# Sums over partitions as four 32-column matmuls, attention spread over all eight convolutions, y's parts made inside the last one

## The chip, the cores and the metric

The kernel runs on one core of a Trainium2 chip. The metric is the device time of one execution in microseconds (us), and lower is better. Where this text speaks of engines, PE is the matrix engine (TensorE), PEld its weight loads, DVE the vector engine, ACT the scalar engine, POOL the GpSimd engine and SP the engine that issues most DMAs. A time that differs by less than 0.2% (4.4 us) cannot be told from no change by this measurement.

## The reference

One transformer block for 512 tokens of width 2048 in float32: a normalised and modulated input goes through one wide projection. A third of the projection's columns feed a gated short convolution, the rest a sparse attention. Both outputs are normalised in groups of 128 channels, concatenated, multiplied by `w_out`, gated by `g_a` and added to `x`; a gated feed-forward network (FFN) follows.

```python
sh_a, sc_a, g_a, sh_f, sc_f, g_f = split(silu(c) @ ada_w + ada_b, 6)      # 6 x 2048 columns
h = rms_norm(x, norm_mix) * (1 + sc_a) + sh_a
proj = h @ w_in                                # 512 x 5656
cb, cc, ch, q, kc, vc, ... = split(proj)       # cb, cc, ch: 1024 columns each
u = cc * ch
y_conv = cb * (causal convolution over 3 tokens of u with conv_w)
y_conv = rms_norm(y_conv in 8 groups of 128 channels) * out_norm_conv
y_attn = nsa_mixer(...)                        # 8 heads of 128
y_attn = rms_norm(y_attn per head) * out_norm_attn
x = x + g_a * (concat(y_conv, y_attn) @ w_out)            # w_out 2048 x 2048
h = rms_norm(x, norm_ffn) * (1 + sc_f) + sh_f
x = x + g_f * ((silu(h @ ffn_w1) * (h @ ffn_w3)) @ ffn_w2)
```

## The kernel before

Every float32 product of the projection, of `w_out` and of the FFN is made of three faster matmuls: an operand is split into a high part (`hi`, rounded on ACT) and a low part (`lo`, the rest, subtracted on DVE), and hi·lo, lo·hi and hi·hi are summed in PSUM (`mm3`, L98 to L100). Small products (attention's scores, values and transposes, sums over partitions) are plain float32 matmuls, which the trace shows as two records each.

The stage that the change touches runs from the eight convolutions to the end of `w_out`.

- `conv(c)`, for c from 0 to 7, computes 128 channels of the three gates for all tokens. Its loop goes over 16 chunks of `w_in` in 8 steps of two: SP loads the raw chunk, ACT rounds it (L814), DVE makes its low part (L815, a ring of 3 buffers), and PE does 18 matmuls into three `main` banks. Behind the loop stand the convolution itself on DVE (L826 to L831, L831 being the last reader of the third bank), a square on ACT (L834), the sum of the squares over the 128 partitions by a matmul with a matrix of ones (L836, 512 columns, the sum in all 128 rows), a square root on ACT and a reciprocal on DVE over 128x512 (L123, L124), and the scaling of y (L840).
- `attention_steps()` is a list of 40 steps, of which 37 hold work: scores, softmax, transposes (L769), values (L778), the norm of a head and its turn into `oT` (L798). `weave(..., 0.68)` gives 0.68 of such a step to each of the 64 convolution steps. At that rate the 37 steps are used up in the seventh convolution, and the eighth has none beside it.
- `gates_beside()` multiplies columns of `ada_w` by the conditioning vector on DVE (L190, 128x512 each, from a ring of two buffers `araw` that SP fills) in 152 steps, 2.4 of them beside each convolution step. Where a part of the gate is wanted as a row or in all partitions, its accumulator is summed over partitions by a matmul with ones: L413 (one output row, for the FFN's gate `gfd`, four times, three of them in this stage and one in the fourth `w_out` block) and L211 (`ada_bcast`, all 128 rows, for each of the four `w_out` blocks).
- Then y, in 16 chunks of 128 channels (0 to 7 from the convolutions in `yc`, 8 to 15 from attention in `oT`), is split into its parts, 32 ACT casts (L864) and 32 DVE subtractions (L866) of 128x256. Those of chunks 0 to 6 are tied behind the last convolution's end by `issue_after`.
- `w_out` runs in four blocks of 512 output columns, each over 8 pairs of chunks (24 matmuls a pair), in the order 8 to 15, 0 to 7, with four `main` banks. `beside_block` accumulates the next block's gate beside it and calls `ada_bcast` for its own, and `residual` uses that at the block's end.

There are four `main` and four `aux` PSUM banks. The instructions are recorded in the order of the code and then moved by a scheduler inside the framework, engine by engine; so the order on an engine is not the order of the code. The FFN behind `w_out` takes the rest of the time and is not touched.

Of the kernel before, what the change touches and what calls it, by code (L numbers as in the profile page):

```python
# [9 lines left out]
F32 = mybir.dt.float32  # L10
# [3 lines left out]
ALU = mybir.AluOpType  # L14
# [55 lines left out]
def block_kernel(ctx: ExitStack, tc: tile.TileContext, a: dict, out: bass.AP):  # L70
# [134 lines left out]
            g0 = at[("norm_mix", "norm_ffn")[which]] + k0  # L205
            nc.vector.scalar_tensor_tensor(d, d, 1.0, cols[:, g0:g0 + n], op0=ALU.add, op1=ALU.mult)

    def ada_bcast(psum_tile, dst, acc):

        ps = psum_tile()  # L210
        nc.tensor.matmul(ps, ones, acc, start=True, stop=True)  # L211
        nc.scalar.copy(dst, ps)

    pp = pool("ps", 4, space=PSUM)
    main = lambda: pp.tile([P, S], F32, tag="main", name="main")
# [180 lines left out]

    dram = ctx.enter_context(tc.tile_pool(name="spill", bufs=1, space=bass.MemoryType.DRAM))
    gfd = dram.tile([1, D], F32, name="gfd")
    wst = ExitStack()
    wring = pool("aring", 2, stack=wst)  # L400

    def ffn_part(ring_, width, j):

        got = []
        if j < 8:
            m, j = 1 - j % 2, j // 2
            yield from ada(ring_, width, (3 + m) * D + j * 512, 512, got)
            ada_cols(aux, got[0], 1, m, 4 * j, 4)
        else:
            cs = slice((j - 8) * 512, (j - 7) * 512)  # L410
            yield from ada(ring_, width, 5 * D + cs.start, 512, got, bias=True)
            ps = aux()
            nc.tensor.matmul(ps[0:1, :], ones[:, 0:1], got[0], start=True, stop=True)  # L413
            nc.scalar.copy(got[0][0:1, :], ps[0:1, :])
            nc.gpsimd.dma_start(gfd[:, cs], got[0][0:1, :])
        yield

    def ffn_parts(ring_, width, js):
# [120 lines left out]
    def h_tok(k, i):  # L539
        return [h[:, i * P:(i + 1) * P] for h in hT[k]]  # L540

    every = list(range(KC))


    cst = ExitStack()
# [252 lines left out]
        nc.vector.tensor_mul(oT[:, g * R:(g + 1) * R, i * P:(i + 1) * P], pt.rearrange("p (h t) -> p h t", h=R), gain)  # L798


    conv_ins = [None]

    def conv(c):
        pst = {b: main() for b in (1, 2, 0)}
        for k in range(0, KC, 2):
            raw = ring[0].tile([P, 1024], F32, tag="raw", name="raw")
            hi = ring[1].tile([P, 1024], F32R, tag="hi", name="whi")
            lo = ring[2].tile([P, 1024], F32R, tag="lo", name="wlo")
            m = 2 * 3 * P
            src = w_in[k * P:(k + 2) * P, 0:3 * 1024].rearrange("(k p) (b n) -> p k b n", p=P, b=3)  # L810
            rv = raw[:, :m].rearrange("p (k b n) -> p k b n", k=2, b=3)
            for kk in range(2):
                nc.sync.dma_start(rv[:, kk], src[:, kk, :, c * P:(c + 1) * P])
            nc.scalar.copy(hi[:, :m], raw[:, :m])  # L814
            nc.vector.tensor_sub(lo[:, :m], raw[:, :m], hi[:, :m].bitcast(F32))  # L815
            for b in (1, 2, 0):
                for kk in range(2):
                    s = slice((kk * 3 + b) * P, (kk * 3 + b + 1) * P)
                    mm3(pst[b], [hi[:, s], lo[:, s]], hT[k + kk], k + kk == 0, k + kk == KC - 1)
            yield  # L820
# [10 lines left out]
        conv_ins[-1] = nc.vector.tensor_mul(y, y, pst[0]).ins  # L831

        sq = ap_.tile([P, S], F32, tag="cc", name="cc", bufs=1)
        nc.scalar.activation(sq, y, AF.Square)  # L834
        ps = aux()
        nc.tensor.matmul(ps, ones, sq, start=True, stop=True)  # L836
        rs = ap_.tile([P, S + 2], F32, tag="u", name="u", bufs=1)[:, :S]
        rsqrt(rs, ps, P)
        gain = cols[:, at["out_norm_conv"] + c:at["out_norm_conv"] + c + 1]
        nc.vector.scalar_tensor_tensor(y, y, gain, rs, op0=ALU.mult, op1=ALU.mult)  # L840

    def convs():
        for c in range(8):
# [6 lines left out]
        yield from ada(wring, 512, 2 * D, 512, acc_g, bias=True)  # L850

    later = gates_beside()
    weave(beside(convs(), later, 2.4), attention_steps(), 0.68)
    for _ in later:
        pass

    HS, HK = S // 2, KC // 2
    yT = [None] * KC
    for k in list(range(8, KC)) + list(range(8)):
        src = oT[:, k - 8, :] if k >= 8 else yc[:, k, :]  # L860
        yT[k] = parts()
        for h, t in enumerate(yT[k]):
            part = src[:, h * HS:(h + 1) * HS]
            nc.scalar.copy(t[:, 0:HS], part)  # L864
            with tc.issue_after(conv_ins[-1]) if k < 7 else ExitStack():
                nc.vector.tensor_sub(t[:, HS:S], part, t[:, 0:HS].bitcast(F32))  # L866
    at_.close()
    qk.close()
    wst.close()
# [58 lines left out]
    def beside_block(n, ga):  # L928

        own = acc_g[-1]  # L930
        side = ffn_part(aring, 1024, 11)
        if n < 3:
            side = ada(aring, 1024, 2 * D + (n + 1) * 512, 512, acc_g, bias=True)
        for t, _ in enumerate(after_taken(side)):
            if t == 0:
                if n:
                    x2_turned(n - 1)
                ada_bcast(aux, ga, own)
                if 0 < n < 3:
                    x_load(n + 1)  # L940
            yield
# [90 lines left out]
    for n in range(4):  # L1032
        ga = tp.tile([P, 512], F32, tag="ga", name="ga")
        pst = [main() for _ in range(NT)]
        if n < 3:
            weave(token_block(w_out, n * 512, y_tok, every[8:] + every[:8], pst), beside_block(n, ga), 1)
            residual(n, ga, pst, range(NT))

    def first_half():
# [5 lines left out]

    rbs = dp.tile([P, S], F32, tag="d1", name="rbs")

    weave(last_block_steps(every[8:] + every[:8], pst, first_half), beside_block(3, ga), 2)
    residual(3, ga, pst, range(2, NT))

    def second_half():
# [555 lines left out]
```

## Time and profile before

| what | value |
|---|---|
| median of three runs | 2211.52 us (2209.48 to 2212.58) |
| the profiled execution: its own time | 2209.06 us |
| its span, first to last instruction | 2207.3 us |
| mean granted PE clock | 0.997 of full speed |
| PE, DVE, ACT, POOL busy, share of the span | 98%, 78%, 45%, 10% |
| convolutions and attention, from the first whole step to the first `w_out` matmul | 312 to 721.4 us of the span |
| four `w_out` blocks | 721.4 to about 925 us |

The trace is one execution. Its busy times are those of the records; a PE record's end is modelled, so starts of neighbouring matmuls, not lengths, tell what a matmul costs. An engine works through its instructions in order: whatever stands behind a waiting instruction waits too.

### The profile page before, as it was taken

Reading aid. Unit: us, or ns where it says so; the run is one execution under the profiler, and the core shown is the slowest. Engines: PE = TensorE matmul, PEld = TensorE weight load, DVE = VectorE, ACT = ScalarE, POOL = GpSimd, SP = SyncE. Lnnn points to the kernel's source line nnn. Section 1 sums busy time; section 2 is a strip of 40 time slices with the busy share of each in tenths; the row PEclk is TensorE's granted clock in tenths of the full one; section 3 lists DMA queues with packets and bytes.
Section 4 is the critical chain, followed back from the end, with each engine's and each line's share of the span. In section 5 each row is a group of like instructions: output and inputs, shape, how many; then the busy total and the mean of one; then the engine's idle time right before and its main releaser. Section 6 shows DMA issues by size and latency. Waiting matters only on the chain.

```text
span 2207.3 us, 30666 instructions
## 1 busy us (share of the span) xinstructions
PE 2162.6 (98%) x11393; PEld 1807.2 (82%) x11393; DVE 1731.6 (78%) x2561; ACT 1002.4 (45%) x1594; POOL 225.9 (10%) x273
## 2 busy tenths in 40 slices
PE   6999999999999999999999999999999999999999
PEld 5778777778777788888888888888888887888887
DVE  6777868887877656698778888788788887878788
ACT  5335234555444333654444444444444455454543
POOL 5310000000000000000000000000000112121110
PEclk9999999999999999999999999999999999999999
DMA  9965775645547766269777677777677499797975
GB/s 319 363 232 160 244 234 172 179 147 169 159 142 244 207 244 223 86 160 222 174 185 177 175 170 170 177 186 174 173 167 175 97 314 275 161 292 145 290 161 143
DMA packets 437722, 435.21 MB, mean 197 GB/s; under 512 B 18084, under 2 KB 344588, under 8 KB 436932
## 3 DMA queue, kind: packets, MB, share of 16 engines
q1 hardware_dynamic: 368196, 318.47, 46.3%
q0 software_dynamic: 69232, 114.51, 24.3%
q8 instruction: 89, 1.46, 0.3%
q14 instruction: 61, 0.50, 0.1%
q10 hardware_dynamic: 144, 0.26, 0.0%
HBM read 413.25 MB, written 19.93 MB: 196 GB/s over the span
## 4 chain that ended last, share of the span: by engine, by line
PE 78%; DMA 11%; DVE 8%; issue 1%; ACT 1%; SPq 0%; DVEq 0%; POOL 0%; ACTq 0%; POOLq 0%
PE main L1104 15%; PE aux L1104 11%; DMA araw<-in_ada_w 10%; PE aux L1462 9%; PE main L1462 9%; PE main L1106 8%; PE aux L1106 6%; PE main L98 4%; PE main L100 4%; PE main L99 4%; DVE acc L190 2%; PE aux L98 1%; PE aux L100 1%; PE aux L99 1%; PE aux L778 1%
## 5 line engine op out<-in xcount | busy, mean ns | idle before, releaser
L1090 ACT CAST whi<-raw 128x1024 fp32r<-128x1024 f32 x246 | 257.6, 1047 | 284.3 <-PE main L1104 110.1
L1104 PE MATMUL main<-hC,whi 128*128 128x512 f32 x1408 | 353.5, 392 | 1.4 <-ACT whi L1090 1.4
L1090 ACT CAST whi<-t 128x1024 fp32r<-128x1024 f32 x186 | 195.2, 1050 | 265.1 <-PE aux L1104 70.3
L1097 DVE TENSOR_TENSOR wlo<-raw,whi 128x1024 fp32r<-128x1024 f32 x218 | 266.1, 1221 | 53.7 <-ACT whi L1090 51.3
L1104 PEld LDWEIGHTS main<-hC,whi 128*128 128x128 f32 x1408 | 253.3, 189 | 47.6 <-ACT whi L1090 1.6
L1104 PE MATMUL aux<-hC,whi 128*128 128x512 f32 x1072 | 268.9, 392 | 0.0
L190 DVE SCALAR_TENSOR_TENSOR acc<-araw,cT,acc 128x512 f32<-128x512 f32 x248 | 185.8, 749 | 80.8 <-DMA araw<-in_ada_w 77.1
L1104 PEld LDWEIGHTS aux<-hC,whi 128*128 128x128 f32 x1072 | 192.9, 189 | 34.4
L1106 PEld LDWEIGHTS main<-hC,wlo 128*128 128x128 f32 x1408 | 192.0, 190 | 13.6
L1106 PE MATMUL main<-hC,wlo 128*128 128x256 f32 x1408 | 196.3, 282 | 0.0
L98 PE MATMUL main<-alo,whi 128*128 128x512 f32 x448 | 180.9, 405 | 1.4 <-DVE alo L352 1.4
L99 PE MATMUL main<-ahi,wlo 128*128 128x512 f32 x448 | 176.0, 393 | 0.0
L100 PE MATMUL main<-ahi,whi 128*128 128x512 f32 x448 | 175.6, 393 | 0.0
L92 ACT CAST whi<-raw 128x1024 fp32r<-128x1024 f32 (+2 forms) x84 | 79.2, 948 | 199.3 <-PE main L100 129.7
L1106 PEld LDWEIGHTS aux<-hC,wlo 128*128 128x128 f32 x1072 | 146.3, 190 | 10.4
L1106 PE MATMUL aux<-hC,wlo 128*128 128x256 f32 x1072 | 149.6, 282 | 0.0
L1434 DVE TENSOR_TENSOR wlo<-t,whi 128x1024 fp32r<-128x1024 f32 x102 | 124.4, 1222 | 28.7 <-ACT whi L1090 28.6
L93 DVE TENSOR_TENSOR wlo<-raw,whi 128x1024 fp32r<-128x1024 f32 (+2 forms) x84 | 91.4, 1094 | 68.3 <-ACT whi L92 63.6
L1080 POOL DMA_DIRECT2D t<-in_ffn_w x42 | 65.0, 1547 | 766.4 <-DVE d L1111 581.7
L1097 DVE TENSOR_TENSOR wlo<-t,whi 128x1024 fp32r<-128x1024 f32 x84 | 102.6, 1221 | 38.2 <-ACT whi L1090 37.1
L1462 PE MATMUL main<-wlo,ghi 128*128 128x512 f32 x304 | 118.5, 390 | 1.8 <-DVE wlo L1434 1.8
L1462 PE MATMUL aux<-whi,glo 128*128 128x512 f32 x308 | 119.8, 389 | 0.0
(347 smaller groups left out, 4219.4 us busy)
## 6 DMA issues: line engine op xcount, KB each, us to landing
raw<-in_ffn_w SPq DMA_DIRECT2D x204, 512.0 KB
araw<-in_ada_w SPq DMA_DIRECT2D x192, 256.0 KB
t<-in_ffn_w POOLq DMA_DIRECT2D x90, 512.0 KB, 7.6
t<-in_ffn_w SPq DMA_DIRECT2D x78, 512.0 KB
araw<-in_ada_w POOLq DMA_DIRECT2D x56, 512.0 KB, 14.5
raw<-in_w_in SPq DMA_DIRECT2D x128, 192.0 KB
raw<-in_w_in SPq DMA_DIRECT2D x37, 512.0 KB
araw<-in_ada_w SPq DMA_DIRECT2D x32, 512.0 KB
```

The costliest lines, as they stand in the source:

```text
L92: nc.scalar.copy(hi[:, :m], raw[:, :m])
L93: nc.vector.tensor_sub(lo[:, :m], raw[:, :m], hi[:, :m].bitcast(F32))
L98: nc.tensor.matmul(ps, lhs[0], rhs[1], start=first, stop=False)
L99: nc.tensor.matmul(ps, lhs[1], rhs[0], start=False, stop=False)
L100: nc.tensor.matmul(ps, lhs[0], rhs[0], start=False, stop=last)
L190: nc.vector.scalar_tensor_tensor(acc, w, s, acc, op0=ALU.mult, op1=ALU.add)
L1090: hi_ins[-1] = nc.scalar.copy(hi, t).ins
L1097: lo_ins[-1] = nc.vector.tensor_sub(lo, t, hi.bitcast(F32)).ins
L1104: nc.tensor.matmul(ps, wt[0][:, ks[k]], hc(p, k), start=first and k == 0, stop=False, skip_group_check=True)
L1106: nc.tensor.matmul(ps[:, HS:], wt[1][:, ks[k]], hc(p, k)[:, 0:HS], start=False, stop=last and k == HK - 1, skip_group_check=True)
L1434: W["last"] = nc.vector.tensor_sub(lo, t, hi.bitcast(F32)).ins
L1462: nc.tensor.matmul(ps[2 * t + c], x_[:, j, tok], w[:, cs], start=m == 0 and j == 0 and p in (1, 5, 2), stop=m == 2 and j == GS[b] - 1 and ...
```

## The change

1. **Sums in quarters.** `quarters(t)` replaces the three matmuls with ones over 512 columns. It makes four matmuls with 32 columns of ones: quarter j of the 512 columns goes to rows 32j to 32j+31 of a 128x128 result. So the sum no longer stands in every partition: it lies in four rows, 0, 32, 64 and 96. `row_of` writes these by a POOL DMA to a row in DRAM, and where all partitions need it a second POOL DMA reads it back into 128 partitions (`rs` for y's norm, `ga` for the `w_out` blocks). The square root and the reciprocal of y's norm work on 128x128 where they worked on 128x512. y's scaling waits in a list and is recorded in the fourth step (k = 6) of the next convolution; the last one's behind the convolutions.
2. **Attention at 0.575 of a step** per convolution step, which reaches into the eighth convolution; the gates at 2.3.
3. **y's parts inside the last convolution**: chunks 8 to 11 and 0 to 6 in its steps, 12 to 15 and 7 behind it, and the ties to the convolution's end are gone.
4. **`w_out`'s chunks in that order**: 8 to 11, 0 to 5, 12 to 15, 6, 7.

```diff
+    def quarters(t):
+        ps = aux()
+        for j in range(4):
+            nc.tensor.matmul(ps[32 * j:32 * j + 32, :P], ones[:, 0:32], t[:, j * P:(j + 1) * P], start=True, stop=True,
+                             skip_group_check=True)
+        return ps[:, :P]
+    def row_of(row, t):
+        nc.gpsimd.dma_start(row.rearrange("o (j t) -> (o j) t", j=4), t[0:P:32, :P])
-    def ada_bcast(psum_tile, dst, acc):
-        ps = psum_tile()
-        nc.tensor.matmul(ps, ones, acc, start=True, stop=True)
-        nc.scalar.copy(dst, ps)
+    def ada_bcast(row, small, dst, acc):
+        nc.scalar.copy(small, quarters(acc))
+        row_of(row, small)
+        nc.gpsimd.dma_start(dst, row.to_broadcast([P, 512]))
...
-            nc.tensor.matmul(ps[0:1, :], ones[:, 0:1], got[0], start=True, stop=True)
-            nc.scalar.copy(got[0][0:1, :], ps[0:1, :])
-            nc.gpsimd.dma_start(gfd[:, cs], got[0][0:1, :])
+            nc.scalar.copy(got[0][:, :P], quarters(got[0]))
+            row_of(gfd[:, cs], got[0])
...
+    y_order = every[8:12] + every[0:6] + every[12:16] + every[6:8]
...
         for k in range(0, KC, 2):
+            if k == 6:
+                scale_y()
+            if c == 7:
+                y_parts(((), (8, 9), (10, 11), (0, 1), (2, 3), (4, 5), (6,), ())[k // 2])
...
-        ps = aux()
-        nc.tensor.matmul(ps, ones, sq, start=True, stop=True)
-        rs = ap_.tile([P, S + 2], F32, tag="u", name="u", bufs=1)[:, :S]
-        rsqrt(rs, ps, P)
+        r = ap_.tile([P, S + 2], F32, tag="u", name="u", bufs=1)[:, :P]
+        rsqrt(r, quarters(sq), P)
+        row_of(rsd[c], r)
+        rs = ap_.tile([P, S], F32, tag="cc", name="cc", bufs=1)
+        nc.gpsimd.dma_start(rs, rsd[c].to_broadcast([P, S]))
...
-        nc.vector.scalar_tensor_tensor(y, y, gain, rs, op0=ALU.mult, op1=ALU.mult)
+        scaled_later.append((y, gain, rs))
...
-    weave(beside(convs(), later, 2.4), attention_steps(), 0.68)
+    weave(beside(convs(), later, 2.3), attention_steps(), 0.575)
...
+    y_parts(range(12, 16))
+    scale_y()
+    y_parts((7,))
...
-            weave(token_block(w_out, n * 512, y_tok, every[8:] + every[:8], pst), beside_block(n, ga), 1)
+            weave(token_block(w_out, n * 512, y_tok, y_order, pst), beside_block(n, ga), 1)
```

How the instructions stand on three engines. On PE, the two sums at the start of the last convolution before (L836 sums the squares of convolution 6, L413 a part of the FFN's gate; `main<-alo,whi` and its two companions are the convolution's three matmuls):

```order
L98 MATMUL main<-alo,whi 128x512
L99 MATMUL main<-ahi,wlo 128x512
L100 MATMUL main<-ahi,whi 128x512
L836 MATMUL aux<-cc,const 128x512
L413 MATMUL aux<-acc,const 1x512
L98 MATMUL main<-alo,whi 128x512
L99 MATMUL main<-ahi,wlo 128x512
```

and the second of them now, in the middle of the last convolution:

```order
L100 MATMUL main<-ahi,whi 128x512
L212 MATMUL aux<-acc,const 32x128 x4
L782 MATMUL aux<-const,pr 128x128 x8
L791 MATMUL aux<-vv_1859,pr 128x128 x4
L791 MATMUL aux<-vv_1860,pr 128x128 x4
L98 MATMUL main<-alo,whi 128x512
```

The sum is four matmuls of 32 rows by 128 columns (L212), and attention's transposes (L782) and values (L791) now stand in the last convolution, which had none.

On DVE, between the reciprocal for the norm of y and the scaling that uses it, in the fourth convolution before (both are in the list above as L124 and L840):

```order
L124 RECIPROCAL u<-u 128x512
L761 RECIPROCAL sm<-sm 128x2
L781 SCALAR_TENSOR_TENSOR o_4787<-aux,sm,o_4787 128x128
L840 SCALAR_TENSOR_TENSOR yc<-yc,cols,u 128x512
L762 TENSOR_TENSOR sm<-sm,gts 128x2
```

and now (L190 is the gates' accumulation, L842 a convolution's low part, L768 and L769 belong to attention's scores, L874 is the scaling):

```order
L124 RECIPROCAL u<-u 128x128
L190 SCALAR_TENSOR_TENSOR acc<-araw,cT,acc 128x512
L842 TENSOR_TENSOR wlo<-raw,whi 128x768
L190 SCALAR_TENSOR_TENSOR acc<-araw,cT,acc 128x512
L851 MEMSET u 128x2
L190 SCALAR_TENSOR_TENSOR acc<-araw,cT,acc 128x512
L768 TENSOR_TENSOR aux<-aux,masks 128x256
L842 TENSOR_TENSOR wlo<-raw,whi 128x768
L769 TENSOR_REDUCE nm<-aux 128x2
L874 SCALAR_TENSOR_TENSOR yc<-yc,cols,cc 128x512
L190 SCALAR_TENSOR_TENSOR acc<-araw,cT,acc 128x512
```

The scheduler has put the scaling eight instructions behind the reciprocal, not at the fourth step where the code records it, and it now reads `cc`, the tile that the second DMA fills.

On SP, the first loads of `w_out` before (`x` is the residual's input, 1 MB a load; `araw` of 128x2x512 are the gate's columns for the second block):

```order
L91 DMA raw<-in_w_out 128x2x512
L917 DMA x_6887<-in_x 128x4x512
L917 DMA x_6889<-in_x 128x4x512
L91 DMA raw<-in_w_out 128x2x512 x2
L184 DMA araw<-in_ada_w 128x2x512
L91 DMA raw<-in_w_out 128x2x512
```

and now:

```order
L91 DMA raw<-in_w_out 128x2x512
L184 DMA araw<-in_ada_w 128x512
L91 DMA raw<-in_w_out 128x2x512 x2
L180 DMA acc<-in_ada_b 1x512
L945 DMA x_6956<-in_x 128x4x512
L945 DMA x_6958<-in_x 128x4x512
L184 DMA araw<-in_ada_w 128x2x512 x3
L91 DMA raw<-in_w_out 128x2x512 x2
```

Three chunks of `w_out` now stand ahead of the two loads of `x`, and three gate loads between these and the fourth chunk.

More of the change, by code (lines that the diff above doesn't have):

```diff
@@ L398, in block_kernel @@
     gfd = dram.tile([1, D], F32, name="gfd")
+    gad = [dram.tile([1, 512], F32, name=f"gad{n}") for n in range(4)]
+    rsd = [dram.tile([1, S], F32, name=f"rsd{c}") for c in range(8)]
     wst = ExitStack()
@@ L540, in h_tok @@
         return [h[:, i * P:(i + 1) * P] for h in hT[k]]
+    HS, HK = S // 2, KC // 2
     every = list(range(KC))
+    y_order = every[8:12] + every[0:6] + every[12:16] + every[6:8]
     cst = ExitStack()
@@ L798, in head_turn, with y_parts @@
         nc.vector.tensor_mul(oT[:, g * R:(g + 1) * R, i * P:(i + 1) * P], pt.rearrange("p (h t) -> p h t", h=R), gain)
-    conv_ins = [None]
+    yT = [None] * KC
+    def y_parts(ks):
+        for k in ks:
+            src = oT[:, k - 8, :] if k >= 8 else yc[:, k, :]
+            yT[k] = parts()
+            for h, t in enumerate(yT[k]):
+                part = src[:, h * HS:(h + 1) * HS]
+                nc.scalar.copy(t[:, 0:HS], part)
+                nc.vector.tensor_sub(t[:, HS:S], part, t[:, 0:HS].bitcast(F32))
     def conv(c):
@@ L830, in conv, with scale_y @@
         nc.vector.scalar_tensor_tensor(y, u[:, 0:S], cw(0), y, op0=ALU.mult, op1=ALU.add)
-        conv_ins[-1] = nc.vector.tensor_mul(y, y, pst[0]).ins
+        nc.vector.tensor_mul(y, y, pst[0])
         sq = ap_.tile([P, S], F32, tag="cc", name="cc", bufs=1)
         nc.scalar.activation(sq, y, AF.Square)
-        ps = aux()
-        nc.tensor.matmul(ps, ones, sq, start=True, stop=True)
-        rs = ap_.tile([P, S + 2], F32, tag="u", name="u", bufs=1)[:, :S]
-        rsqrt(rs, ps, P)
-        gain = cols[:, at["out_norm_conv"] + c:at["out_norm_conv"] + c + 1]
-        nc.vector.scalar_tensor_tensor(y, y, gain, rs, op0=ALU.mult, op1=ALU.mult)
+        r = ap_.tile([P, S + 2], F32, tag="u", name="u", bufs=1)[:, :P]
[3 more added lines that the diff above has]
+        nc.gpsimd.dma_start(rs, rsd[c].to_broadcast([P, S]))
+        gain = cols[:, at["out_norm_conv"] + c:at["out_norm_conv"] + c + 1]
+        scaled_later.append((y, gain, rs))
+    scaled_later = []
+    def scale_y():
+        for y, gain, rs in scaled_later:
+            nc.vector.scalar_tensor_tensor(y, y, gain, rs, op0=ALU.mult, op1=ALU.mult)
+        scaled_later.clear()
     def convs():
@@ L852, in block_kernel @@
     later = gates_beside()
-    weave(beside(convs(), later, 2.4), attention_steps(), 0.68)
+    weave(beside(convs(), later, 2.3), attention_steps(), 0.575)
     for _ in later:
         pass
[L857 to L866, printed above, removed]
+    y_parts(range(12, 16))
+    scale_y()
+    y_parts((7,))
     at_.close()
@@ L937, in beside_block @@
                     x2_turned(n - 1)
-                ada_bcast(aux, ga, own)
+                ada_bcast(gad[n], tp.tile([P, P], F32, tag="dg", name="dg"), ga, own)
                 if 0 < n < 3:
@@ L1046, in block_kernel @@
     rbs = dp.tile([P, S], F32, tag="d1", name="rbs")
-    weave(last_block_steps(every[8:] + every[:8], pst, first_half), beside_block(3, ga), 2)
+    weave(last_block_steps(y_order, pst, first_half), beside_block(3, ga), 2)
     residual(3, ga, pst, range(2, NT))
```

## The prediction

> **What bounds the kernel now.** I read the page's busy times and its chain first, then the table of stages, then PE's own waits in the stage that is changed.
>
> ```profile
> PE 2162.6 (98%) x11393; PEld 1807.2 (82%) x11393; DVE 1731.6 (78%) x2561; ACT 1002.4 (45%) x1594; POOL 225.9 (10%) x273
> PE 78%; DMA 11%; DVE 8%; issue 1%; ACT 1%; SPq 0%; DVEq 0%; POOL 0%; ACTq 0%; POOLq 0%
> ```
>
> ```profile
> 312.00:721.40 409.40, 402.02 (x2008) 321.58 (x2007) 325.92 (x659) 200.67 (x459) 4.14 (x8) 1.00 0.58 174
> 690.00:729.00 39.00, 37.00 (x156) 28.69 (x156) 34.82 (x58) 19.86 (x40) 1.01 (x2) 1.00 0.81 272
> 729.00:780.00 51.00, 51.00 (x229) 41.53 (x228) 31.94 (x44) 16.82 (x26) 5.59 (x6) 1.00 0.73 205
> 830.00:880.00 50.00, 50.00 (x227) 41.12 (x227) 29.98 (x38) 15.01 (x23) 1.44 (x2) 1.00 0.65 221
> ```
>
> ```profile
> PE aux L836 <- ACT cc L834: 3.1, 2, 2.5
> PE aux L727 <- ACT pr L760: 1.6, 3, 1.0
> PE aux L778 <- DVE shf L201: 1.1, 1, 1.1
> PE main L98 <- DVE yc L831: 0.6, 1, 0.6
> PE aux L769 <- DVE gsc L201: 0.5, 1, 0.5
> PE aux L778 <- ACT pr L760: 0.4, 2, 0.3
> ```
>
> The columns of the stages are length, then busy time of PE, PEld, DVE, ACT and POOL, the granted clock, the DMA engines' share and GB/s. The first row is the convolutions with attention: PE is busy 402.0 of 409.4 us, DVE 325.9 (80%). The second is the end of the last convolution: DVE 34.8 of 39.0 (89%). In the `w_out` rows PE has no gap at all. The waits (355 to 735 us, each with total, times and longest) are all that PE shows: 3.1 + 1.6 + 1.1 + 0.6 + 0.5 + 0.4 = 7.3 us. So the stage is bound by PE, and an edit can win in two ways only: by taking work off PE, which counts in full, or by removing some of these 7.3 us. DVE, DMA and POOL matter as far as they make PE wait.
>
> The Trainium skill ("Trainium Kernel Development and Optimization", Performance Expectations) calls matmul busy time a bad measure and the busy share of weight loads a good one. By that rule the stage is less full than its 98% says; what this would give is a rival below, worked from the PEld column.
>
> **The sums.** Sixteen sums over partitions are replaced: eight for y's norm (L836), four for the blocks' gates (L211), four for the FFN's gate (L413). Their price on PE is what they put between the convolution's matmuls.
>
> ```profile
> 729.55 0.40 PE L100 MATMUL main<-whi,alo 128*128 128x512 f32 x1
> 729.79 1.02 PE L211 MATMUL aux<-acc,const 128*128 128x512 f32 x2
> 730.24 0.79 PE L100 MATMUL main<-whi,ahi 128*128 128x512 f32 x1
> 730.88 0.40 PE L98 MATMUL main<-wlo,ahi 128*128 128x512 f32 x1
> 731.11 0.39 PE L99 MATMUL main<-whi,ahi 128*128 128x512 f32 x1
> ```
>
> ```profile
> 887.63 0.40 PE L100 MATMUL main<-whi,ahi 128*128 128x512 f32 x1
> 887.96 1.02 PE L413 MATMUL aux<-acc,const 128*1 128x512 f32 x2
> ...
> 889.25 0.40 PE L99 MATMUL main<-whi,ahi 128*128 128x512 f32 x1
> ```
>
> ```profile
> 105.97 0.39 PE L100 MATMUL aux<-ahi,whi 128*128 128x512 f32 x1
> 106.28 1.96 PE L281 MATMUL aux<-araw,crep 128*32 128x128 f32 x64
> 108.06 0.40 PE L281 MATMUL aux<-acc,const 128*32 128x128 f32 x8
> 108.39 0.50 PE L98 MATMUL aux<-wlo,ahi 128*128 128x512 f32 x1
> 108.72 0.41 PE L99 MATMUL aux<-whi,alo 128*128 128x512 f32 x1
> ```
>
> Undisturbed matmuls start 0.23 us apart (730.88 to 731.11). From the start at 729.55 to that at 730.88 pass 1.33 us, of which two steps (0.46) would pass without the sum: a 128-row sum costs 0.87. By the same sum the one-row L413 costs 889.25 - 887.63 - 0.46 = 1.16, that is 0.29 more for the same 512 columns. I read the 0.29 as the price of changing to a narrow part of the array and back, since it is the only difference of form (128*1 for 128*128). The new form already runs in the kernel's first stage: L281 makes 32-row, 128-column products in four quarters, and its eight records of `acc` with `const` are exactly one `quarters`. The whole group of 72 records, 36 matmuls, costs 108.72 - 105.97 - 0.46 = 2.29; less 0.29 for the change that is 2.00/36 = 0.056 each. One `quarters` alone then costs 4 x 0.056 + 0.29 = 0.51.
>
> So L836 and L211 win 0.87 - 0.51 = 0.36 each, twelve times 4.3 us; L413 wins 1.16 - 0.51 = 0.65, four times 2.6 us: 6.9 us, all on PE's path. The upper end takes what the trace shows at the start of the next matmul (108.06 to 108.39, 0.33 us): 12 x 0.54 + 4 x 0.83 = 9.8. The lower end is that the four do not overlap when they stand alone and cost a whole sum and the change: 12 x -0.29 + 0 = 3.5 us lost. I take 6.9, which is nearest to the row of the same form.
>
> The Trainium skill ("TensorEngine Tiling (Array Packing)", Key Properties) says that changing the tiling mode drains the array, while different tiles work in parallel. That rule speaks against twelve of these edits, which put two changes where there was none; the trace agrees in kind, as far as the 0.29 us of L413 can show it, and at this price the overlap still wins. By the drain alone the sum would be the lower end, 3.5 us lost; with the overlap of the L281 rows it is 6.9 won.
>
> **DVE, and the way through DRAM.** The reciprocal goes from 512 to 128 elements per partition.
>
> ```profile
> L124 DVE RECIPROCAL u<-u 128x512 f32<-128x512 f32 x8 | 26.8, 3346 | 0.0
> L124 DVE RECIPROCAL ssa<-ssa 128x4 f32<-128x4 f32 x8 | 1.3, 168 | 0.5 <-ACT ssa L123 0.5
> ```
>
> ```profile
> araw<-in_ada_w POOLq DMA_DIRECT2D x56, 512.0 KB, 14.5
> k<-gd POOLq DMA_DIRECT2D x44, 256.0 KB, 7.5
> out<-x POOLq DMA_DIRECT2D x6, 512.0 KB, 3.4
> gfd<-acc POOLq DMA_DIRECT2D x4, 2.0 KB, 1.9
> ```
>
> A line through the two rows gives (3346 - 168)/508 = 6.3 ns an element, so 0.94 us: 2.4 saved, eight times, 19 us of DVE. It counts only where PE waits for DVE. Against it stands a new wait: the scaling needs the row in all partitions, and in the fourth convolution it stands on DVE behind three accumulations of the gates, two low parts and two instructions of attention, of which these rows price the first five:
>
> ```profile
> L190 DVE SCALAR_TENSOR_TENSOR acc<-araw,cT,acc 128x512 f32<-128x512 f32 x248 | 185.8, 749 | 80.8 <-DMA araw<-in_ada_w 77.1 <-issue 0.9
> L815 DVE TENSOR_TENSOR wlo<-raw,whi 128x768 fp32r<-128x768 f32 x64 | 61.0, 953 | 8.5 <-ACT whi L814 8.2
> L866 DVE TENSOR_TENSOR ahi<-oT,ahi 128x256 fp32r<-128x256 f32 x8 | 3.3, 422 | 0.0
> ```
>
> 3 x 0.75 + 2 x 0.95 = 4.2 us, on a DVE that is busy 80% of the time 5.2. The row takes about 0.5 to issue (an estimate: POOL's busy 1.0 us for two instructions in the second stage row) and 1.9 to land, the broadcast of 256 KB again 0.5 and between 3.4 and 7.5 (a store and the loads of POOL's queue): 6.3 to 10.4 us. So DVE waits there between 1 and 5 us. Behind it stand the gates, attention's next scores and the next low parts; PE meanwhile has the convolution's matmuls (18 x 0.23 = 4.1 us a step) between two steps of attention, 4.1/0.575 = 7.1 us. DVE is held about as long as the old reciprocal held it (3.3 us), under the same cover, and I book neither gain nor loss for that; where the cover fails, it is a rival. On POOL the second DMA waits for the first, and behind it stand only the fills of accumulators that are needed a part later. The blocks' `ga` takes the same way, some 10 us, and is used at the end of a block of 8 pairs of chunks, 8 x 24 x 0.23 = 44 us.
>
> **The spread.** The last convolution had two sums (0.87 + 1.16) beside its 144 matmuls (33 us). Now 24 transposes, 32 value products and 4 score products of attention stand there:
>
> ```profile
> L778 PE MATMUL aux<-vv,pr 128*128 128x128 f32 x320 | 41.6, 277 | 1.6 <-DVE shf L201 1.1 <-ACT pr L760 0.4
> L769 PE MATMUL aux<-const,pr 128*128 128x128 f32 x160 | 23.3, 273 | 0.5 <-DVE gsc L201 0.5
> L750 PE MATMUL aux<-kT,qT 128*128 128x512 f32 x32 | 15.1, 594 | 0.0
> ```
>
> 24 x 23.3/160 + 32 x 41.6/160 + 4 x 15.1/16 (two records to a product) = 3.5 + 8.3 + 3.8 = 15.6 us of PE work, taken from the other convolutions. DVE gets the time for it: 25 subtractions of y's parts (0.42 each, 10.5 us) where 16 stood. For the sums over the eight convolutions nothing changes. What can change are the waits:
>
> ```profile
> 684.36 1.54 DVE L190 SCALAR_TENSOR_TENSOR acc<-araw,cT,acc 128x512 f32<-128x512 f32 x2 [1.42 <-DMA araw<-in_ada_w]
> 691.38 1.12 PE L836 MATMUL aux<-cc,const 128*128 128x512 f32 x2 [2.45 <-ACT cc L834]
> 715.36 0.75 DVE L190 SCALAR_TENSOR_TENSOR acc<-araw,cT,acc 128x512 f32<-128x512 f32 x1 [3.12 <-DMA araw<-in_ada_w]
> ```
>
> The longest of PE's waits, 2.45 us, stands where DVE was crowded at the start of the last convolution, itself held by a gate load. The four rows of L727, L778 and L769 (3.6 us) wait for attention's chain through DVE and ACT, which now has 0.68/0.575 = 1.18 times the convolution work between its steps. I expect half of 7.3 to go, 3.6, and take off 1.3 for new waits of the same kind at new places: 2.3 us. Ends: 7.3, and a loss of 3.1, the wait of the third row, if a gate load stands in front of the last convolution's tail and holds its third bank from `w_out`.
>
> **Edits at nothing.** `w_out`'s order: a pair is 24 x 0.23 = 5.5 us, so chunks 12 to 15 are wanted five pairs (27 us) after the convolutions; if they were late, PE would wait at the sixth pair. The gates at 2.3 leave five steps behind the convolutions in the code; in the order they end ahead of the last convolution's tail, and their sum is wanted only at the end of the first block. The two loads of `x` and the first gate load (2.5 MB, at the 272 GB/s of the second stage row 9.2 us) go out behind `w_out`'s third chunk, whose buffer comes free when the low part of the last step but one is made, so at least two steps (8.2 us) before the convolution's last matmul: short by 1 us at worst, or the 3.1 that the trace shows.
>
> **The sum.** 6.9 + 2.3 = 9.2 us. On the profiled execution's own time, 2209.06 - 9.2 = 2199.9; the median of the runs lies 2.5 higher, so 2211.5 - 9.2 = 2202.3. The case's own range is 2199 to 2206.
>
> **The rivals.**
> - *Only the sums pay*: new waits of attention and of the scaling replace the old one for one. 2211.5 - 6.9 = 2204.6. For it: the 7.3 us are spread over ten small events.
> - *All waits go*: 2211.5 - 6.9 - 7.3 = 2197.3, with the cheapest `quarters` 2194.4. For it: weight loads fill 41.53/51.0 = 81.4% of a `w_out` stage and 321.58/409.4 = 78.5% of the convolutions, so at that density the stage would be 14.3 us shorter, and busy records may hide waits. Against: the small float32 matmuls load less per us. This is where the rule of the Trainium skill on weight loads would take the time.
> - *The quarters win nothing* because alone they drain and do not overlap: 2211.5 - 2.3 = 2209.2, no change. Against: 36 of them in 2.29 us.
> - *The way through DRAM holds DVE* (the other side), at the scaling of seven convolutions. If the broadcast lands as late as the first of the DMA rows, 14.5 us, the way takes 17.4, DVE waits 17.4 - 5.2 = 12.2, PE's cover of 7.1 fails by 5.1, seven times 36 us: 2211.5 - 6.9 + 36 = 2240.6. It turns the result from a wait of 7.1 + 6.9/7 = 8.1 on, a landing of 10.4. Against: that row is from the start, where the DMA engines were full; in this stage their share is 0.58.
>
> **How the numbers follow.** Forecast 0.52, only the sums 0.16, all waits 0.16, no gain 0.08, DRAM 0.08. The first three lie over 4.4 us (0.2%) below 2211.5, so faster 0.84, same 0.08, slower 0.08. The range runs from the second rival's lower end, 2194.4, to the third's 2209.2; it leaves out the fourth.
>
> **What would show it.** Right: L212's records in place of L836 put about 0.5 us between neighbouring starts; L124 over 128x128 at 0.9 us; PE's idle in the stage below 7; the `w_out` blocks about 0.4 us shorter each. Wrong: DVE waiting for `cc<-rsd` by more than 4 us a time, PE waiting for low parts behind it, or the fourth tile of `w_out`'s first pair waiting for L858 by over 3 us.

## The result and the profile after

The changed kernel takes 2201.59 us (median of 6 runs, 2196.12 to 2202.45), the kernel before 2212.05 in the same comparison (2209.48 to 2219.38): ratio 0.9947, 95% interval 0.9935 to 0.9960. By the medians that is 10.5 us less, by the interval 8.8 to 14.4. 2202.3 was forecast. The profiled execution took 2202.23 us, its span is 2200.5. The number is right, and so is its largest term, the sums. The other terms are not: the spread wins nothing by itself, and DVE's time was not free. That the total fits all the same is in part luck. (Of the twelve executions of `e9_long_reciprocal`, below, one took 2627 us at a granted clock of 0.766; the ratio leaves it out.)

First the page's busy times and chain, then the table of stages of the changed kernel (length, busy time of PE, PEld, DVE, ACT and POOL, granted clock, DMA share, GB/s), the first three rows placed as in the table before, but 3 to 4 us earlier.

```profile
PE 2157.7 (98%) x11489; PEld 1805.8 (82%) x11489; DVE 1715.6 (78%) x2561; ACT 999.5 (45%) x1596; POOL 239.4 (11%) x297
PE 80%; DMA 10%; DVE 7%; issue 1%; ACT 1%; SPq 0%; DVEq 0%; POOL 0%; ACTq 0%; POOLq 0%
```

```profile
309.00:717.90 408.90, 400.87 (x2064) 322.61 (x2063) 309.05 (x659) 198.21 (x457) 12.25 (x22) 0.99 0.60 175
686.00:725.00 39.00, 38.61 (x214) 31.77 (x212) 27.39 (x54) 21.11 (x45) 1.07 (x2) 1.00 0.62 217
725.00:776.00 51.00, 51.00 (x245) 41.75 (x244) 33.22 (x46) 16.73 (x29) 8.31 (x11) 1.00 0.89 266
```

The second row is the end of the last convolution: DVE is busy 27.4 of 39 us, where it was 34.8. That is not the work of the spread alone: at the same place it is busy 29.9 us in the kernel with the sums alone, and 28.8 in the one with the spread alone (both below). The first row has DVE 16.9 us lower than before, PE nearly as busy, and, what no row before had, a granted clock below 1.00. PE's waits (355 to 735 us) say how little is gained in them:

```profile
PE aux L212 <- ACT cc L861: 2.3, 1, 2.3
PE aux L740 <- ACT pr L773: 2.2, 1, 2.2
PE aux L791 <- ACT pr L773: 2.0, 3, 0.9
PE aux L791 <- DVE shf L201: 0.3, 1, 0.3
```

6.8 us, where 7.3 stood (with one of 0.9 ahead of 355 us, 7.7 in the whole stage; below 7 was forecast). The wait at the start of the last convolution (2.45) and the one at the seam to `w_out` (0.62) are gone; two of 2.3 and 2.2 us stand at new places. Now the sums, at the place in `w_out` that the prediction measured, and the rows of the way through DRAM on DVE:

```profile
724.90 0.40 PE L100 MATMUL main<-whi,alo 128*128 128x512 f32 x1
725.23 0.43 PE L212 MATMUL aux<-acc,const 128*32 128x128 f32 x8
725.59 0.50 PE L98 MATMUL main<-wlo,ahi 128*128 128x512 f32 x1
725.93 0.40 PE L99 MATMUL main<-whi,ahi 128*128 128x512 f32 x1
```

```profile
L190 DVE SCALAR_TENSOR_TENSOR acc<-araw,cT,acc 128x512 f32<-128x512 f32 x248 | 185.7, 749 | 66.4 <-DMA araw<-in_ada_w 63.5
L124 DVE RECIPROCAL u<-u 128x128 f32<-128x128 f32 x8 | 7.6, 948 | 1.2 <-ACT u L123 1.0
L874 DVE SCALAR_TENSOR_TENSOR yc<-yc,cols,cc 128x512 f32<-128x512 f32 x8 | 6.0, 751 | 10.3 <-DMA cc<-rsd 10.2
```

One `quarters` costs 725.93 - 724.90 - 2 x 0.23 = 0.57 us (0.51 forecast; the old sum 0.87). The reciprocal takes 0.95 (0.94 forecast). DVE waits 10.2 us in all for the broadcast rows, and at most 2.7 at a time. Store and broadcast land (median, us) after

```profile
cc<-rsd POOLq DMA_DIRECT2D x8, 256.0 KB, 4.5
rsd<-u POOLq DMA_DIRECT2D x8, 2.0 KB, 2.2
```

**Where the time went, stage by stage.** The starts and waits of PE's rows give this table. Both kernels' stage is cut at the same two matmuls (327.07 to 721.41 us before; 324.38 to 717.95 after). The `w_out` row ends at the 720th of its 768 matmuls into `main`, 897.2 us before (the last one starts at 910.2, so the "about 925" of the table of the kernel before is too late). "Half clock" is what PE lost to the granted clock (busy time times what the clock lacked to 1, in steps of 2 us); "rest" is PE at full clock without waits. The third column is a second trace of the changed kernel (`after_again`, below).

| us | before | after | after, again |
|---|---|---|---|
| start, up to the stage | 327.1 | 324.4 | 322.7 |
| stage: PE's waits | 7.3 | 7.7 | 6.1 |
| stage: half clock | 0 | 3.2 | 1.7 |
| stage: rest | 387.0 | 382.6 | 381.4 |
| `w_out`, 720 matmuls: waits / rest | 0.6 / 175.2 | 0 / 172.8 | 0 / 172.7 |
| behind it | 1310.1 | 1309.7 | 1309.4 |

The rest falls by 4.4 in the stage and 2.4 in `w_out`: 6.8 us, the sums (5.6 + 2.5 = 8.1 by the second trace). All traces of this document say the same: stage and `w_out` together, the rest is 562.2 and 563.8 us in the two kernels with the old sums, and 552.9 to 555.9 in the twelve with quarters. The waits do not fall. The start, in which the instructions of PE, DVE and ACT stand in the same order in both kernels, differs by 2.7 to 4.4 us; of its 327.1, 324.4 and 322.7 us, 4.8, 3.0 and 1.6 are half clock. So a pair of traces carries that much of chance, and the parts must be judged by the timed runs.

### The profile page after: what moved, and what is told of

Read it like the earlier page. It is cut to its first block, busy times and chain, and to the rows that moved or that the text cites. A ratio compares the mean times of both kernels' runs of the same rounds, so it can differ in the third digit from the quotient of the medians.

```text
span 2200.5 us, 30924 instructions
## 1 busy us (share of the span) xinstructions
PE 2157.7 (98%) x11489; PEld 1805.8 (82%) x11489; DVE 1715.6 (78%) x2561; ACT 999.5 (45%) x1596; POOL 239.4 (11%) x297
## 4 chain that ended last, share of the span: by engine, by line
PE 80%; DMA 10%; DVE 7%; issue 1%; ACT 1%; SPq 0%; DVEq 0%; POOL 0%; ACTq 0%; POOLq 0%
PE main L1132 15%; PE aux L1132 11%; PE aux L1490 9%; PE main L1490 9%; DMA araw<-in_ada_w 9%; PE main L1134 8%; PE aux L1134 6%; PE main L98 5%; PE main L100 5%; PE main L99 5%; DVE acc L190 2%; PE aux L791 1%; PE aux L98 1%; PE aux L100 1%; PE aux L99 1%
## 5 line engine op out<-in xcount | busy, mean ns | idle before, releaser
L190 DVE SCALAR_TENSOR_TENSOR acc<-araw,cT,acc 128x512 f32<-128x512 f32 x248 | 185.7, 749 | 66.4 <-DMA araw<-in_ada_w 63.5
L1462 DVE TENSOR_TENSOR wlo<-t,whi 128x1024 fp32r<-128x1024 f32 x102 | 124.1, 1219 | 28.8 <-ACT whi L1118 28.7
L1490 PE MATMUL aux<-whi,ghi 128*128 128x512 f32 x308 | 119.8, 389 | 0.0
```

Of the source, the lines that this page charges most:

```text
L190: nc.vector.scalar_tensor_tensor(acc, w, s, acc, op0=ALU.mult, op1=ALU.add)
L1462: W["last"] = nc.vector.tensor_sub(lo, t, hi.bitcast(F32)).ins
L1490: nc.tensor.matmul(ps[2 * t + c], x_[:, j, tok], w[:, cs], start=m == 0 and j == 0 and p in (1, 5, 2), stop=m == 2 and j == GS[b] - 1 and ...
```

## The experiments

Behind the first comparison, the kernels were timed in three groups (e1 to e4; the changed kernel again and e5 to e7; e8 to e11). Each has its own runs of the kernel before, 2209.15, 2205.71 and 2208.22 us, and the differences are the ratio to these, in us. The first group ran on one chip, the other two on another; the changed kernel itself is in the second alone, so what is said of e8 to e11 against it goes by two ratios.

| kernel | median, us | ratio (95% interval) | difference |
|---|---|---|---|
| changed, first comparison | 2201.59 | 0.9947 (0.9935 to 0.9960) | -11.7 |
| e1_sums_only | 2204.80 | 0.9981 (0.9969 to 0.9992) | -4.2 |
| e2_spread_only | 2210.14 | 1.0005 (0.9996 to 1.0014) | +1.1 |
| e3_old_rates | 2199.99 | 0.9959 (0.9947 to 0.9970) | -9.1 |
| e4_late_sums | 2200.20 | 0.9962 (0.9950 to 0.9973) | -8.4 |
| after_again: changed | 2195.89 | 0.9956 (0.9943 to 0.9968) | -9.7 |
| e5_scale_late | 2194.37 | 0.9947 (0.9934 to 0.9961) | -11.7 |
| e6_three_hops | 2200.27 | 0.9976 (0.9967 to 0.9985) | -5.3 |
| e7_parts_after | 2198.79 | 0.9970 (0.9959 to 0.9981) | -6.6 |
| e8_gates_loaded_once | 2182.07 | 0.9880 (0.9867 to 0.9893) | -26.5 |
| e9_long_reciprocal | 2208.58 | 0.9992 (0.9981 to 1.0002) | -1.8 |
| e10_gates_slower | 2199.63 | 0.9961 (0.9947 to 0.9976) | -8.6 |
| e11_sums_scale_late | 2207.42 | 0.9994 (0.9985 to 1.0003) | -1.3 |

An interval is 2 to 3 us to each side.

### The parts apart

`e1_sums_only`, from the changed kernel:

```diff
-            if c == 7:
-                y_parts(((), (8, 9), (10, 11), (0, 1), (2, 3), (4, 5), (6,), ())[k // 2])
...
-    weave(beside(convs(), later, 2.3), attention_steps(), 0.575)
+    weave(beside(convs(), later, 2.4), attention_steps(), 0.68)
-    y_parts(range(12, 16))
     scale_y()
-    y_parts((7,))
+    for k in list(range(8, KC)) + list(range(8)):
...
-    y_order = every[8:12] + every[0:6] + every[12:16] + every[6:8]
+    y_order = every[8:] + every[:8]
```

> The sums in quarters with their way through DRAM, but attention's steps at the old rates (0.68 and 2.4), y's parts all after the convolutions and w_out's chunks in the old order. The prediction's step on the sums: 6.9 us below the kernel before. Rival, the sums win nothing and the spread makes the whole difference: 0 to 1 us below. Rival, the sums win the whole difference: 10 us below. In the trace PE's largest wait at the start of the last convolution (2.45 us before) stays.

`e2_spread_only`: the three sums of the kernel before, in the changed kernel.

```diff
-        rsqrt(r, quarters(sq), P)
-        row_of(rsd[c], r)
...
+        ps = aux()
+        nc.tensor.matmul(ps, ones, sq, start=True, stop=True)
+        rsqrt(rs, ps, P)
+        nc.vector.scalar_tensor_tensor(y, y, gain, rs, op0=ALU.mult, op1=ALU.mult)
```

> The old sums over 512 columns with the old scaling, but the new rates, y's parts inside the last convolution and the new order in w_out. The prediction's step on the spread: 2.3 us below the kernel before. Rival, waits only change their place: 0 to 0.6 (the wait at the seam to w_out). Rival, the spread makes what the sums don't: 10.5 - 6.9 = 3.6 us below.

The sums alone win 4.2 of the 6.9 us, the spread alone wins nothing, and both together 10: the parts don't add. PE's full-clock time is as forecast in both (383.1 + 172.9 us for the sums alone, 388.3 + 175.5 for the spread). What differs are the waits. With the sums alone, PE's rows at the seam to `w_out`, and the clock behind them:

```profile
689.32 0.42 PE L212 MATMUL aux<-cc,const 128*32 128x128 f32 x8 [2.48 <-ACT cc L860]
722.76 0.50 PE L98 MATMUL main<-wlo,alo 128*128 128x512 f32 x1 [1.36 <-DVE u L852]
728.81 0.80 PE L98 MATMUL main<-wlo,alo 128*128 128x512 f32 x1 [3.04 <-DVE yc L857]
```

```profile
728.00:730.00 2.00, 1.19 (x6) 0.54 (x8) 2.00 (x6) 0.64 (x1) 0.00 (x0) 0.69 0.84 265
730.00:732.00 2.00, 2.00 (x13) 1.33 (x12) 1.35 (x4) 0.37 (x1) 0.00 (x0) 0.50 0.68 242
```

`w_out`'s third and fourth tiles wait 4.4 us for the banks that the last convolution's tail on DVE still reads (0.62 before), and then start at half clock. (This execution took 2209.32 us, 4.5 more than the median, so it may show more waits than most.) With the spread alone the seam is free, but PE waits more for attention's chain and for the squares (all waits from 323 to 898 us):

```profile
PE aux L865 <- ACT cc L863: 3.9, 3, 2.9
PE aux L742 <- ACT pr L775: 3.3, 3, 1.9
PE aux L793 <- ACT pr L775: 2.3, 5, 0.8
```

With two of 0.9 these are 11.3 us in the stage, where 7.3 stood. Two more kernels fill the square of rates and parts, both with the sums in quarters: `e3_old_rates` is the changed kernel with the first edit, `e7_parts_after` the sums alone with the second:

```diff
-    weave(beside(convs(), later, 2.3), attention_steps(), 0.575)
+    weave(beside(convs(), later, 2.4), attention_steps(), 0.68)
```

```diff
-    weave(beside(convs(), later, 2.4), attention_steps(), 0.68)
+    weave(beside(convs(), later, 2.3), attention_steps(), 0.575)
```

> The changed kernel with the two rates back at 0.68 and 2.4; all else as changed. If the rates are what thins attention's waits, PE's waits in the stage come back toward 7.3 and more, and the time is 2 to 3 us above the changed kernel's (2201.6). If waits only change their place, it is the same within 1 us.

> Quarters and the new rates, but y's parts all behind the convolutions and w_out's old order: with the changed kernel, the one with old rates and the one with the sums alone it makes a square of rates and parts. If the parts inside the last convolution are what removes the wait at the seam to w_out (4.4 us with the sums alone, 0 in the changed kernel), it stands 3 to 6 us above the changed kernel. If the rate of the gates is (2.3 leaves their last steps behind the convolutions), it stands within 1 us of it.

Old rates, parts after: -4.2. Old rates, parts inside: -9.1. New rates, parts after: -6.6. Both: -9.7 and -11.7. ("Parts inside" has `w_out`'s new order with it.) By these the parts inside the last convolution are worth 3 to 5 us, and the new rates 2.4 without them, which the intervals do not part from nothing. The traces follow at the seam: PE waits there 4.7 us with neither, 2.0 with the parts alone, 0.8 with the rates alone (for a weight's low part, no longer for a bank), 0 with both.

### What DVE's time is worth

> The changed kernel once more, as the measure for the others of this chip: 8 to 11 us below the kernel before. If idle times of PE near 2 us bring TensorE's half clock in some executions and not in others, this trace has it at other places than the first one (62, 302 and 374 us).

9.7 us below, with half clock at 52 and 438 us in place of 62, 301 and 373: the same kernel, other places. `e9_long_reciprocal` gives DVE back nearly what the narrow reciprocal saved, and `e8_gates_loaded_once` leaves out most gate loads, and with them the right gates; it keeps every instruction of DVE and PE, though not in the same order:

```diff
         rsqrt(r, quarters(sq), P)
+        for _ in range(2):
+            nc.vector.reciprocal(r, r)
```

> The changed kernel with three reciprocals of the row in place of one (the last two cancel out): 2 x 0.95 = 1.9 us more of DVE at each of eight sums, 15 us in all, nearly what the narrow reciprocal saved. The prediction booked that saving at nothing. If it is nothing, the time is within 1 us of the changed kernel. If it is what lets the spread pay (the spread with the old sums won nothing), PE's waits in the stage rise by 3 to 4 us and the time with them.

```diff
-            raw = ring.tile([P, width], F32, tag="araw", name="araw")
...
+            if width > 512 or k0 < 2 * step:
+                raw = ring.tile([P, width], F32, tag="araw", name="araw")
...
```

> The changed kernel, but each gate made beside the convolutions loads only its first two of 16 pieces and multiplies the second one for the rest, so 14 of 16 gate loads (and right gates) are left out; every instruction of DVE and PE stays. In the changed kernel DVE waits 39 us for gate loads, and PE's two large waits (at 371 and 437 us) stand behind DVE instructions queued behind such waits. If gate loads cause them, PE's waits in the stage fall from 6 to 8 us to under 3, the half clock behind them goes too, and the time is 4 to 7 us below the changed kernel. If DVE's own work causes them, the waits stay and the time is within 1.5 us of it.

The ratio with the long reciprocal is 0.9992 (0.9981 to 1.0002) against 0.9956 (0.9943 to 0.9968) of the changed kernel: 7.9 us for 15 us of DVE's work, 2.9 to 13 by the ends of the intervals. Its PE waits (324 to 735 us):

```profile
PE aux L740 <- ACT pr L773: 3.8, 2, 2.2
PE aux L791 <- DVE shf L201: 3.4, 1, 3.4
PE aux L212 <- ACT cc L861: 3.1, 2, 2.9
PE aux L791 <- ACT pr L773: 2.6, 4, 0.9
PE aux L782 <- DVE sc L721: 1.0, 1, 1.0
```

14.7 us with a smaller one, and 4.6 lost at half clock, while PE's full-clock time is the same (382.4). So DVE's time in this stage is not free, although DVE is busy only three quarters of it. What a microsecond of its work costs is not shown, because the kernel differs in more than the work: the row now comes later, and DVE waits more for it. These are DVE's waits for the broadcast rows in the changed kernel again, with the long reciprocal, and with three more copies on the way (`e6_three_hops`, below):

```profile
DVE yc L874 <- DMA cc<-rsd: 9.5, 7, 2.5
DVE yc L876 <- DMA cc<-rsd: 17.3, 7, 4.4
DVE yc L877 <- DMA cc<-hop: 17.5, 8, 6.3
```

The long reciprocal adds 15 us of work and 7.8 of waits, 23 in all, of which 7.9, a third, come out; the three copies add 8.0 of waits alone, and 4.4 come out. The scheduler also moved some 86 of the 636 instructions that DVE has in the stage for the long reciprocal, and 35 for the copies, so these rates are estimates. Without the gate loads, all that PE waits in the stage is this:

```profile
PE aux L741 <- ACT pr L774: 0.7, 2, 0.4
```

By the ratios the time is 16.8 us below the changed kernel, where 4 to 7 were expected. Against the trace of `after_again`, 8.4 lie in the stage (380.8 for 389.2 us: 5.4 of waits, 1.7 of half clock, 1.3 of the rest) and 6.4 in the start, which makes its last gates the same way. How a gate load reaches PE is seen on DVE ahead of PE's wait at 373 us in the changed kernel:

```profile
369.40 0.75 DVE L190 SCALAR_TENSOR_TENSOR acc<-araw,cT,acc 128x512 f32<-128x512 f32 x1 [1.05 <-DMA araw<-in_ada_w]
370.07 0.75 DVE L857 SCALAR_TENSOR_TENSOR yc<-u,cols,yc 128x512 f32<-128x512 f32 x1
370.73 0.95 DVE L842 TENSOR_TENSOR wlo<-raw,whi 128x768 fp32r<-128x768 f32 x1
371.60 0.68 DVE L858 TENSOR_TENSOR yc<-yc,main 128x512 f32<-128x512 f32 x1
```

The last two steps of the first convolution's y stand on DVE behind an accumulation that waits 1.05 us for its load; the square on ACT follows, then PE's sum (373.06). By these rows the load explains 1.05 us of PE's wait of 2.30; the rest is the other work that stands on DVE in front of the two steps. Nearly all of PE's waits in the stage go with these loads (0.7 us is left), so the loads are the most likely cause behind them. That they are the only one is not shown: without them the scheduler set DVE and PE in another order, some 150 of the 619 instructions that DVE then has in the stage. `e10_gates_slower` takes a part of the gates out of the stage, and scales y as late as `e5_scale_late`, below:

```diff
-            if k == 6:
+            if k == 10:
...
-    weave(beside(convs(), later, 2.3), attention_steps(), 0.575)
+    weave(beside(convs(), later, 2.0), attention_steps(), 0.575)
```

> The changed kernel with the gates at 2.0 steps for 2.3, so 24 of 152 gate steps come after the convolutions, and with y scaled two pairs later. If DVE's waits for gate loads set PE's waits, one seventh of them goes, about 1 us, and the time is 1 to 3 us below the changed kernel, unless the gates left over hold the seam to w_out: then PE waits there by 2 to 5 us and the time is as much above it.

The stage gets shorter (386.6 us, waits 4.7), and the gates left over hold the seam and the first block's sum (waits of 1.3 and 2.0 us, and half clock, 1.7): -8.6 in all, no better than the changed kernel.

### The way through DRAM

`e5_scale_late` is the changed kernel and `e11_sums_scale_late` the sums alone with the first edit below, `e4_late_sums` has the second, and `e6_three_hops`, the third, lengthens the way:

```diff
-            if k == 6:
+            if k == 10:
                 scale_y()
```

```diff
-            if k == 6:
+            if k == 2:
+                sum_y()
+            if k == 8:
                 scale_y()
...
-        rsqrt(r, quarters(sq), P)
...
+        summed_later.append((c, y, sq))
```

```diff
         row_of(rsd[c], r)
+        for n in range(3):
+            nc.gpsimd.dma_start(hops[3 * c + n], hops[3 * c + n - 1] if n else rsd[c])
         rs = ap_.tile([P, S], F32, tag="cc", name="cc", bufs=1)
-        nc.gpsimd.dma_start(rs, rsd[c].to_broadcast([P, S]))
+        nc.gpsimd.dma_start(rs, hops[3 * c + 2].to_broadcast([P, S]))
```

> The changed kernel with y scaled two pairs later (at the sixth pair of the next convolution, for the fourth). DVE's waits for the broadcast (10.2 us in the changed kernel) go to 0 to 2. If PE's cover hides them, as the prediction has it, the time stays within 1 us of the changed kernel; if they are what keeps PE's waits in the stage at 7.7 us, it falls by 2 to 5.

> The changed kernel with three more copies of the row, DRAM to DRAM, between the store and the broadcast; some 2 to 2.5 us each, so 6 to 8 us more on the way. DVE's wait at the scaling grows from 1.7 (10.2 over 6) to 8 or 9 us. By the prediction's fourth rival PE's cover is 7.1 us, so 1 to 2 us a convolution come out, seven times: 7 to 14 us above the changed kernel. If DVE cannot catch up behind a wait at all, all of it counts: 40 to 55 above. If DVE's slack takes it, 0 to 2.

> The changed kernel with the sum of each convolution's squares made a step later (at the second pair of the next convolution) and y scaled at the fifth pair instead of the fourth. In the changed kernel's trace PE idles 2.30 us before the first of these sums, because the square comes late from ACT, and TensorE's granted clock is 0.5 for 6 us behind that idle. If the wait and the half clock are real costs of this place, both go: up to 2.3 + 3 = 5 us below the changed kernel. If such waits come back elsewhere one for one, the same time.

> The sums alone (old rates, y's parts after the convolutions, old order), with y scaled two pairs later. The sums alone gave 4.3 us for 6.9, and DVE waited up to 4.5 us for a broadcast. If that wait is where the missing 2.6 went, it comes out at 6 to 7 us below the kernel before. If it is the seam to w_out (4.4 us of PE's waits there), 4 to 5 below as before.

The place in the code turned out to be a poor handle on the wait. Reciprocal and scaling of the fifth convolution on DVE, in the changed kernel again, in e5 and in e6:

```profile
570.08 0.94 DVE L124 RECIPROCAL u<-u 128x128 f32<-128x128 f32 x1
578.82 0.75 DVE L874 SCALAR_TENSOR_TENSOR yc<-yc,cols,cc 128x512 f32<-128x512 f32 x1 [1.78 <-DMA cc<-rsd]
```

```profile
571.79 0.94 DVE L124 RECIPROCAL u<-u 128x128 f32<-128x128 f32 x1
580.07 0.75 DVE L874 SCALAR_TENSOR_TENSOR yc<-yc,cols,cc 128x512 f32<-128x512 f32 x1
```

```profile
570.12 0.94 DVE L124 RECIPROCAL u<-u 128x128 f32<-128x128 f32 x1
587.21 0.75 DVE L877 SCALAR_TENSOR_TENSOR yc<-yc,cols,cc 128x512 f32<-128x512 f32 x1 [3.32 <-DMA cc<-hop]
```

8.7, 8.3 and 17.1 us lie between them: the scheduler moves the scaling by 8 us for the three hops, and leaves it where it was for the two pairs (it seems to set it where it reckons the row to be there). DVE waits 9.5 us in all in the changed kernel again and 8.3 in e5, where 0 to 2 were expected; in e6 17.5, of which 6.3 are at the row of the last convolution and at most 3.3 at each of the others. So e5 (0.9947, 0.9934 to 0.9961, beside 0.9956 of the changed kernel on that chip) shows no difference, as its first theory had it, but for another reason, and e6 does not put the prediction's turning point (8.1 us of wait) to the test, since at the seven convolutions that it speaks of the longest wait is 3.3. It costs 4.4 us against the changed kernel (the intervals touch), with 9.6 us of PE's waits for 6.1; by which of its effects stays open. e4 gives the same time as the changed kernel within the intervals, and the wait that it was to remove is still there (1.81 us, half clock behind it): a step later the square is late as well. e11 (0.9994 for 0.9981 of the sums alone, the intervals overlap) fell on neither side that it was to tell apart: its waits at the seam (1.1, 1.8 and 2.5 us) are of the kind of e1's, and DVE's wait for the broadcast is not gone either (9.4 us in all, at most 4.9; in e1 11.0 and 4.5). So which of the two takes the missing 2.7 us of the sums alone is not settled by it; the traces show the seam's price, and no PE wait behind the 4.5.

## Why the prediction was right, and where not

- **What bounds the stage.** That an edit can win only on PE's work or on PE's waits held for the sums. The 7.3 us are one execution's waits. As a judgement of DVE it failed: "DVE, DMA and POOL matter as far as they make PE wait" was read as if the rest of DVE's time were slack. By e9 a third of what DVE is held longer comes out, with DVE at 77%; e8, without the gate loads, is 16.8 us faster.
- **The sums.** Right in size and in kind: 6.9 forecast, 4.4 + 2.4 = 6.8 measured on PE's full-clock time (8.1 in the second trace), and the twelve kernels with quarters stand apart from the two without. Each `w_out` block was to be 0.4 us shorter; 2.4 over four is 0.6. One `quarters` is 0.57 for 0.51; the overlap of the four survives alone, so the lower end (the array only drains, 3.5 lost) is out, and the rival of quarters that win nothing with it.
- **The way through DRAM, booked at nothing.** This is a step that failed without hurting the sum. DVE is rid of 26.8 - 7.6 = 19.2 us and waits 10.2 for the rows: 9 us net, by e9 (7.9 us for the 15 of work, or for the 23 with the waits) 3 to 5 us of gain, an estimate. PE's cover was to hide both; by e9 and e6 it hides only a part. The fourth rival's signs did not come: no wait over 2.7 us, the broadcast lands in 4.5 (median).
- **The spread.** 2.3 forecast as half of the old waits less new ones. Alone it wins nothing (e2: 1.0005, 0.9996 to 1.0014), and in the changed kernel's traces the stage's waits are 7.7 and 6.1 for 7.3, plus half clock; new waits came about one for one, as the prediction's first rival (only the sums pay) had it. What the spread does is another thing: it frees the seam that is held in the kernel with the quarters alone (4.7 us of waits and 1.5 of half clock, none in the changed kernel); from that kernel to the changed one are 5.5 us (ratios 0.9981 and 0.9956). The prediction costed it against the kernel before, where the seam cost 0.62.
- **Edits at nothing.** Right: PE has no wait in `w_out`, the fourth tile of its first pair included.
- **The sum.** 9.2 forecast, 11.7 and 9.7 measured. 6.8 to 8.1 of them are the sums; the rest, 2 to 5 us, is not the spread's own 2.3, and where it comes from stays open. DVE's saving and the seam, which only the spread frees, are candidates, but the traces do not show it: PE's waits and half clock, stage and `w_out` together, are 7.9 us before and 10.9 and 7.7 in the two traces of the changed kernel, and what these are shorter by beyond the sums stands in the start, which the change does not touch. Of the kernel before there is one trace; if its stage waited less than most executions do, the missing time is there, but that is not shown. So the total is right by the sums, and for the rest by luck.

No kernel here that keeps its loads beats the changed one by more than the intervals; e5 is 1.5 us below it by the medians, within them.

## What to carry over

An engine that is busy 80% of the time beside a full PE need not be covered. Here DVE's instructions stood behind others that waited for loads, its work came out at PE's waits in part, and the PE waits that an edit removed came back at other places. So trace a PE wait back along the other engine's order to the instruction that really waited, and price a saving on that engine by adding a known amount of work to it; but count what else the added work changes, its later waits and the scheduler's new order. And when two edits go together, try each alone: one may only pay by hiding what the other costs.

## What the runs showed of the hardware

The clock. After some of PE's idle times the granted clock stands at 0.5 for 3.4 or 6.8 us. The first four rows are the changed kernel around its wait of 2.30 us at 371 to 373, the last three the kernel before around its wait of 2.45 us at 689 to 691 (columns as in the table of stages):

```profile
369.73:373.14 3.41, 1.11 (x9) 0.61 (x11) 3.41 (x6) 1.07 (x3) 0.00 (x0) 1.00 0.34 87
373.14:376.55 3.41, 3.41 (x21) 3.03 (x22) 1.63 (x3) 1.54 (x2) 0.00 (x0) 0.50 0.92 270
376.55:379.97 3.42, 3.42 (x13) 2.94 (x12) 3.34 (x10) 2.34 (x7) 0.59 (x1) 0.50 0.34 108
379.97:383.38 3.41, 3.41 (x16) 2.83 (x16) 2.31 (x9) 1.35 (x4) 0.56 (x1) 1.00 0.64 185
```

```profile
686.90:690.32 3.42, 2.03 (x9) 1.31 (x7) 3.38 (x6) 1.12 (x3) 0.00 (x0) 1.00 0.41 136
690.32:693.73 3.41, 2.35 (x6) 0.69 (x7) 3.41 (x8) 2.58 (x5) 0.00 (x0) 1.00 0.83 242
693.73:697.14 3.41, 3.41 (x16) 2.81 (x15) 3.41 (x3) 1.43 (x5) 0.53 (x2) 1.00 0.67 193
```

The first wait costs 3.4 us more at half clock (3.2 in the table's coarser steps), more than the wait itself; the second, longer one costs none. What parts them is where they fall. In each of the fourteen traces all stretches of half clock begin on one grid of 3.413 us and last one step of it or two; the rows above are cut along it. The first wait lies in one step, in which PE is idle for 2.30 us; the second is split, 1.39 and 1.06 us. Cut so from 90 to 2150 us, all 23 steps in which PE's records leave 1.77 us or more idle are followed by half clock, 2 of the 17 between 1.5 and 1.76 are, and none below (four of the 25 went on for a second step). Where the grid lies against the program's start differs from execution to execution, so for a single wait it is a matter of chance: from 90 to 900 us, 21 of 37 idle times of 1.8 us and more were followed by half clock, and 2 of 34 between 1.0 and 1.8, at 1.4 to 3.4 us each. So a wait of 2 us costs about 3 on the mean, and the same program differs from execution to execution by several us. The Trainium skill ("TensorE: Matmul & The Clock Gate", What's actually happening) says that the array falls to half rate after at least one idle window of about 3.4 us, and that the window runs free. The second half fits the grid in these traces. The first does not: a step that was idle for about half its length was enough, 1.54 us once (e5, at 371 us).
